# A two-layer decoder trunk on one core: when the first MLP-down weights are loaded, and where a product's addition stands in VectorE's queue

## The chip, the core and the metric

The kernel runs on one core of one Trainium2 chip. The metric is the time of one launch in microseconds (us) of device time; the figure for a kernel is the median of its runs. One further execution was taken with the profiler, and its rows are the ones read below. Engine names: PE is TensorE (matmuls), DVE is VectorE, ACT is ScalarE, POOL is GpSimd, SP is SyncE, which here only issues transfers (DMAs).

## The reference

The input x is 256 tokens by 2048 features in float32. There are two layers. Each normalises x, passes it through a token mixer (native sparse attention in layer 0, chunked gated linear attention in layer 1), adds the result to x, and then runs the part that the change touches, an MLP with a squared ReLU:

```python
def squared_relu_mlp(h, w_up, w_down):
    return jnp.square(jax.nn.relu(h @ w_up)) @ w_down

for i in range(DEPTH):
    h = rms_norm(x, norm_mix[i])
    ...
    x = x + y.astype(x.dtype)
    h = rms_norm(x, norm_mlp[i])
    x = x + squared_relu_mlp(h, mlp_w_up[i], mlp_w_down[i]).astype(x.dtype)
```

`w_up` is 2048 x 8192 and `w_down` 8192 x 2048 in each layer, all in float32.

## The kernel before, in words

**Weights and their two parts.** Every weight arrives in pieces of 128 x 2048 float32 (1 MB) and is used in two halves of 128 x 1024. For each half ACT writes a high part `wh` (a cast), DVE writes the low part `wl` (weight minus high part), and PE multiplies three ways: high by high, high by low, low by high. `Weights` (line 358) keeps this going. `next` (L489) hands out the half that is used now, and first calls `split` (L432) for the half three uses ahead (`AHEAD`, L359), which issues ACT's cast. The low part is issued later, by `lows` (L469), called from within the matmuls that use the current half. `lows` also issues what may follow a low part: the next transfer into the freed buffer, and the sums below.

**MLP-up** runs in 8 chunks of 1024 hidden columns, each 8 weight pieces, so 16 halves ("U" halves: 8 matmuls of 512 columns and 8 of 256). Pieces come through three buffers `raw`, loaded by SP (L419) as soon as a buffer is free.

**MLP-down** of a chunk, in chunks 0 to 6, is done by a scheme with seven products in place of eight (`Seven`, L863). For a group of four weight blocks a, b, c, d it uses the products `b11, d1, b22, b21, t2, d2, t4`, in this order (L306); their weights are a, b+a, d, c and further running sums of the blocks. The blocks are loaded into five buffers `sraw` by `load_group` (L425, the transfer is L326). The sums are made in place: some by DVE (L200), the others by POOL with an adding DMA from SBUF to SBUF (L337), which is issued from `after_lows` (L343) once the low parts that read the old value are done. Each product has two halves of six matmuls ("S" halves). After its second half, `product` (L873) calls `add` (L859), a DVE instruction that scales the PSUM tile and adds it to a 128 x 512 block of the residual `xt` (L204 in the profile). The products b22, t2, d2 and t4 go on in the PSUM tile of an earlier product, so their first matmul has to wait until that earlier product's `add` has read it.

**Order.** `MIXES` (L516) sets the order by hand: in a chunk, U halves of the next chunk stand between the products of this one (`"UU" + "SUSUSUSUSUUSUS"` twice, where each S is a whole product of two halves). Chunk 0 of MLP-up comes before all of this, with U halves alone; chunk 7 of MLP-down is done plainly. All engines run what stands in their own queue in the order in which the program issues it; other small work (squared ReLU, splits of the hidden values) is slipped in by `W.tick`, from planned costs.

Before chunk 0 of MLP-up, `mlp` (L771) loads the first group's four blocks and the first block of the second group at once, and issues the two sums for `d1`:

```python
weights.load_group(5)
first.sum("d1", 0)
first.sum("d1", 1)
```

Of the kernel before, what the change touches and what calls it, by code (L numbers as in the profile page):

```python
# [10 lines left out]
F32 = mybir.dt.float32  # L11
# [7 lines left out]
P = 128  # L19
T = 256  # L20
# [103 lines left out]
def trunk_kernel(ctx: ExitStack, tc: tile.TileContext, a: dict, out: bass.AP):  # L124
# [6 lines left out]
    def nm(s):  # L131
        uid[0] += 1
        return f"{s}_{uid[0]}"
# [7 lines left out]
    zpool = ctx.enter_context(tc.tile_pool(name="zpool", bufs=1))  # L141
# [16 lines left out]
    def mm(dst, lhsT, rhs, **kw):  # L158
        n = free(rhs)
        if lhsT.dtype == F32R:  # L160
            c = n / 2.4 + 3 if n >= 128 else 107.0
        else:
            c = max(4 * n / 2.4 + 3, 214.0)
        W.run("pe", c, [dst], [lhsT, rhs])
        nc.tensor.matmul(dst, lhsT, rhs, skip_group_check=True, **kw)  # L165
# [7 lines left out]
    def act(dst, src, func, bias=None, scale=None, acc=None):  # L173
        c = free(src) * 0.833 + (60 if in_psum(src) else 100)
        kw = {}
        outs = [dst]
        ins = [src]
        for k, v in (("bias", bias), ("scale", scale)):
            if v is not None:
                kw[k] = v  # L180
                if not isinstance(v, float):
                    c += 95
                    ins.append(v)
        if acc is not None:
            kw["accum_out"] = acc
            outs.append(acc)
            c += 95
        if func in (AF.Exp, AF.Ln, AF.Tanh) and (func == AF.Ln) != table[0]:
            table[0] = func == AF.Ln
            c += 1300  # L190
        W.run("act", c, outs, ins)
        nc.scalar.activation(dst, src, func, **kw)
# [5 lines left out]
    def tt(dst, x, y, op):  # L198
        W.run("dve", free(dst) * 1.042 + 75, [dst], [x, y])
        nc.vector.tensor_tensor(dst, x, y, op=op)  # L200

    def stt(dst, x, s, y, op0, op1):
        W.run("dve", free(dst) * 1.042 + 75, [dst], [x, s, y])
        nc.vector.scalar_tensor_tensor(dst, x, s, y, op0=op0, op1=op1)  # L204
# [8 lines left out]
    def vcopy(dst, src):  # L213
        W.run("dve", free(dst) * (1.042 if in_psum(src) else 0.53) + 75, [dst], [src])
        nc.vector.tensor_copy(dst, src)
# [31 lines left out]
    def aux(shape, dtype=F32):  # L247
        t = paux.tile(shape, dtype, tag="aux", name=nm("psx"))
        W.take("aux", t)
        return t  # L250

    def acc1():
        t = pacc.tile([P, 512], F32, tag="acc", name=nm("psa"))
        W.take("acc", t)
        return t
# [244 lines left out]
    weights = Weights()  # L500
# [17 lines left out]
    def mlp_items(c):  # L518
        return MIXES[SEVENS[c]]
# [159 lines left out]
    class PrepFeatures(Prep):  # L679
# [18 lines left out]

        def squares(self):
            yield 14000.0  # L700
            self.sum = zpool.tile([P, T], F32, tag="sum", name=nm("sum"))
            for kt in range(KT):
                while self.st[kt] is None or not self.st[kt]["done"]:
                    yield 0.0
                yield 0.0, {"aux": 1}
                ps = aux([P, 512])
                act(ps[:, 0:T], xs[kt], AF.Square)
                yield W.ready(ps)
                if kt:
                    tt(self.sum, self.sum, ps[:, 0:T], ALU.add)  # L710
                else:
                    vcopy(self.sum, ps[:, 0:T])
                W.give(ps, W.t["dve"])
# [57 lines left out]
    def mlp(prep, after, last):  # L771
        op = prep.op
        with tc.tile_pool(name="mlpz", bufs=1) as zp:
# [3 lines left out]
            def factors():  # L777

                ms = yield from prep.mean_squares()
                yield W.ready(ms)  # L780
                r2 = small.tile([P, 2, 16], F32, tag="r2", name=nm("r2"), bufs=1)[:, :, 0:NT]
                recip(r2[:, 0, :], ms)
                ts(r2[:, 1, :], r2[:, 0, :], -1.0, None, ALU.mult)
                fac["r2"] = r2
# [70 lines left out]
            def hidden_done():  # L855
                if last_z and not last_z[0]["done"]:
                    W.drain(last_z[0])

            def add(t, b, ps, sign=0):  # L859

                stt(xt[t][b], ps, fac["r2"][:, sign, t:t + 1], xt[t][b], ALU.mult, ALU.add)

            class Seven:  # L863
# [9 lines left out]
                def product(self, name):  # L873
                    if name in ("b11", "d1", "b21"):
                        W.wait({"acc": 1})
                        ps = acc1()
                        if name == "b11":
                            self.x = ps
                        else:
                            self.z = ps  # L880
                    else:
                        ps = self.x if name in ("t2", "d2", "t4") else self.z
                    fresh = name in ("b11", "d1", "b21")
                    for half in range(2):
                        hi, lo = weights.next()
                        for j in range(2):
                            p = 2 * half + j
                            ht = self.pairs[p][0]
                            xh, xl = ht[:, 0, self.A[name], :], ht[:, 1, self.A[name], :]
                            wh, wl = hi[:, j * 512:(j + 1) * 512], lo[:, j * 512:(j + 1) * 512]  # L890
                            mm(ps, xh, wh, start=(fresh and p == 0), stop=False)
                            mm(ps, xh, wl, start=False, stop=False)
                            mm(ps, xl, wh, start=False, stop=(p == 3))
                            if j == 0:
                                weights.lows()
                            W.tick(5000.0)
                    b = self.b
                    for t, k, sign in {"b11": [(0, 0, 0)], "d1": [(1, 1, 1)], "t2": [(0, 1, 1)], "b22": [(0, 1, 1)],
                                       "d2": [(1, 1, 1)], "b21": [(0, 0, 0)], "t4": [(1, 0, 0)]}[name]:
                        add(t, b + k, ps, sign)  # L900
                    if name in ("b22", "b21", "t4"):
                        W.give(ps, W.t["dve"])

# [30 lines left out]

            last_z = []
            weights.pool = zp
            first = weights.sloads[0][0][0]
            weights.load_group(5)
            first.sum("d1", 0)
            first.sum("d1", 1)  # L940
            W.spawn(factors())
            cur = Up(0)
            for f, half in [(0, 0), (1, 0), (0, 1), (1, 1)] + [(f, half) for f in range(2, 8) for half in range(2)]:
                cur.half(f, half)
            for c in range(8):
                items = mlp_items(c)
                nxt = Up(c + 1) if c < 7 else None
                plain = Plain(c, cur.pairs, 2 * SEVENS[c])
                n = {"U": 0, "S": 0, "C": 0}
                for it in items:  # L950
                    i = n[it]
                    n[it] += 1
                    if it == "U":
                        nxt.half(i // 2, i % 2)
                        if c == 6 and i == 15:
                            prep.free()
                    elif it == "S":
                        if i == 0:
                            hidden_done()
                        if i % 7 == 0:  # L960
                            seven = Seven(cur.pairs, 2 * (i // 7))
                        seven.product(Group.ORDER[i % 7])
                    else:
                        plain.half(i)
                cur.free()
                cur = nxt
# [844 lines left out]
    for kt in range(KT):  # L1811
        W.done[W.key(xs[kt])] = (3900.0, 6000.0, 8300.0, 10500.0, 13000.0, 13500.0, 17500.0, 18000.0)[kt // 2]
        preps[0].start(kt)
    nsa(preps[0], preps[1])
    mlp(preps[1], preps[2], False)
    gla(preps[2], preps[3])
    mlp(preps[3], None, True)


# [143 lines left out]
```

## Time and profile before

| | |
|---|---|
| median of 3 runs | 2203.72 us (2202.97, 2203.72, 2207.70) |
| the profiled execution | 2206.16 us, of which the span from the first to the last instruction is 2204.2 us |
| mean granted clock of PE | 0.996 of 2.4 GHz |
| PE busy | 2175.3 us of the span |
| DVE, ACT, POOL busy | 1743.6, 1363.9, 151.4 us |
| moved by DMA | 483.81 MB, mean 219 GB/s |

Times in the rows are counted from the span's start. A row of a list in order of time may stand for several instructions (xcount) and gives their common length; in brackets stands how long the engine was idle just before, and what ended that wait. "PE psx" matmuls are U halves here, "PE psa" matmuls are products. Matmuls overlap in the pipe, so lengths of work are best read as the distance between two starts. Layer 0's MLP runs from about 411 us, layer 1's from about 1510 us.

### The profile page before, as it was taken

Reading aid. Unit: us, or ns where it says so; the run is one execution under the profiler, and the core shown is the slowest. Engines: PE = TensorE matmul, PEld = TensorE weight load, DVE = VectorE, ACT = ScalarE, POOL = GpSimd, SP = SyncE. Lnnn points to the kernel's source line nnn. Section 1 sums busy time; section 2 is a strip of 40 time slices with the busy share of each in tenths; the row PEclk is TensorE's granted clock in tenths of the full one; section 3 lists DMA queues with packets and bytes.
Section 4 is the critical chain, followed back from the end, with each engine's and each line's share of the span. In section 5 each row is a group of like instructions: output and inputs, shape, how many; then the busy total and the mean of one; then the engine's idle time right before and its main releaser. Section 6 shows DMA issues by size and latency. Waiting matters only on the chain.

```text
span 2204.2 us, 29692 instructions
## 1 busy us (share of the span) xinstructions
PE 2175.3 (99%) x11131; PEld 1828.5 (83%) x11131; DVE 1743.6 (79%) x2369; ACT 1363.9 (62%) x2118; POOL 151.4 (7%) x189
## 2 busy tenths in 40 slices
PE   9999999999999999999999999999999999999999
PEld 7888888788888888888888888888888888888887
DVE  6687676589999999998666656655899999998985
ACT  6567776466666666666566555445666666666663
POOL 0010100001001001001000000000000110010010
PEclk9999999999999999999999999999999999999999
DMA  7653452749879879878655354457598798798784
GB/s 259 219 189 134 147 178 96 264 166 282 263 244 274 273 233 280 273 237 230 210 193 180 125 183 153 153 190 252 171 299 255 237 283 263 244 275 266 225 229 153
DMA packets 83087, 483.81 MB, mean 219 GB/s; under 512 B 10496, under 2 KB 13200, under 8 KB 35072
## 3 DMA queue, kind: packets, MB, share of 16 engines
q1 hardware_dynamic: 61264, 403.78, 49.7%
q0 software_dynamic: 21680, 78.15, 18.4%
q8 instruction: 87, 1.43, 0.2%
q14 instruction: 56, 0.46, 0.1%
HBM read 405.35 MB, written 2.10 MB: 185 GB/s over the span
## 4 chain that ended last, share of the span: by engine, by line
PE 94%; DMA 3%; DVE 2%; ACT 1%; issue 0%; SPq 0%; ACTq 0%; DVEq 0%
PE psa L165 58%; PE psx L165 34%; DMA raw<-in_mlp_up_dram 2%; PE psx L169 2%; DVE wl L200 1%; DMA sraw<-sraw 1%; ACT wh L196 0%; DMA raw<-in_nsa_in_dram 0%; DVE xt L204 0%; SPq L326 0%; DVE att L1690 0%; ACT zz L196 0%; DVE sraw L200 0%; DVE pT L200 0%; SPq L1804 0%
## 5 line engine op out<-in xcount | busy, mean ns | idle before, releaser
L165 PE MATMUL psa<-wh,op 128*128 128x512 f32 x2616 | 863.0, 394 | 1.5 <-ACT wh L196 1.5
L200 DVE TENSOR_TENSOR wl<-raw,wh 128x1024 fp32r<-128x1024 f32 (+1 forms) x529 | 641.9, 1219 | 252.6 <-ACT wh L196 248.6
L196 ACT CAST wh<-raw 128x1024 fp32r<-128x1024 f32 (+1 forms) x533 | 557.3, 1047 | 313.1 <-PE psa L165 247.0
L165 PEld LDWEIGHTS psa<-wh,op 128*128 128x128 f32 x2616 | 491.9, 188 | 107.4 <-ACT wh L196 2.5
L200 DVE TENSOR_TENSOR wl<-sraw,wh 128x1024 fp32r<-128x1024 f32 x392 | 475.0, 1221 | 83.5 <-ACT wh L196 81.9
L165 PE MATMUL psx<-op,wh 128*128 128x512 f32 (+1 forms) x2080 | 519.7, 392 | 7.6 <-ACT wh L196 7.6
L165 PE MATMUL psa<-wl,op 128*128 128x512 f32 x1308 | 510.8, 391 | 0.8 <-DVE wl L200 0.8
L196 ACT CAST wh<-sraw 128x1024 fp32r<-128x1024 f32 x392 | 409.5, 1049 | 145.5 <-PE psa L165 86.7
L165 PEld LDWEIGHTS psx<-op,wh 128*128 128x128 f32 (+1 forms) x2080 | 387.2, 189 | 87.6 <-ACT wh L196 8.0
L165 PE MATMUL psa<-wh,ht 128*128 128x512 f32 x1128 | 387.4, 396 | 11.4 <-ACT zz L196 5.5
L165 PEld LDWEIGHTS psx<-op,wl 128*128 128x128 f32 x2048 | 281.0, 191 | 20.3
L165 PE MATMUL psx<-op,wl 128*128 128x256 f32 x2048 | 287.2, 283 | 0.0
L165 PEld LDWEIGHTS psa<-wl,op 128*128 128x128 f32 x1308 | 246.2, 188 | 48.4 <-DVE wl L200 1.5
L165 PEld LDWEIGHTS psa<-wh,ht 128*128 128x128 f32 x1128 | 212.9, 189 | 57.5 <-ACT zz L196 8.4
L165 PE MATMUL psa<-wl,ht 128*128 128x512 f32 x564 | 221.9, 393 | 0.0
L337 POOL DMA_DIRECT2D sraw<-sraw x140 | 120.2, 957 | 1324.7 <-DVE pz L200 485.2
L204 DVE SCALAR_TENSOR_TENSOR xt<-psa,r,xt 128x512 f32<-128x512 f32 x212 | 157.4, 745 | 7.9 <-PE psa L165 7.9
L196 ACT COPY zz<-psx 128x256 f32<-128x256 f32 x128 | 47.7, 373 | 163.2 <-PE psx L165 163.2
L165 PEld LDWEIGHTS psa<-wl,ht 128*128 128x128 f32 x564 | 106.2, 188 | 16.9
L200 DVE TENSOR_TENSOR sraw<-sraw,sraw 128x1024 f32<-128x1024 f32 x84 | 102.6, 1221 | 1.0
L200 DVE TENSOR_TENSOR zz<-psx,zz 128x256 f32<-128x256 f32 x128 | 53.7, 420 | 11.1 <-ACT zz L196 9.9
L196 ACT CAST ht<-pz 128x896 fp32r<-128x896 f32 (+1 forms) x40 | 37.1, 928 | 25.7 <-DVE pz L204 24.7
(195 smaller groups left out, 1206.7 us busy)
## 6 DMA issues: line engine op xcount, KB each, us to landing
raw<-in_mlp_up_dram SPq DMA_DIRECT2D x128, 1024.0 KB, 8.5
sraw<-in_mlp_down_dram SPq DMA_DIRECT2D x112, 1024.0 KB, 11.0
sraw<-sraw POOLq DMA_DIRECT2D x140, 512.0 KB, 9.3
raw<-in_gla_in_dram SPq DMA_DIRECT2D x48, 1024.0 KB, 4.9
raw<-in_nsa_in_dram SPq DMA_DIRECT2D x38, 1024.0 KB, 4.9
raw<-in_nsa_out_dram SPq DMA_DIRECT2D x16, 1024.0 KB, 4.9
raw<-in_mlp_down_dram SPq DMA_DIRECT2D x16, 1024.0 KB, 4.9
raw<-in_gla_out_dram SPq DMA_DIRECT2D x16, 1024.0 KB, 4.8
```

The lines of the kernel that those rows point to most:

```text
L165: nc.tensor.matmul(dst, lhsT, rhs, skip_group_check=True, **kw)
L169: nc.tensor.transpose(dst, src, idn)
L196: nc.scalar.copy(dst, src)
L200: nc.vector.tensor_tensor(dst, x, y, op=op)
L204: nc.vector.scalar_tensor_tensor(dst, x, s, y, op0=op0, op1=op1)
L337: nc.gpsimd.dma_start(dst, src, accum_op=ALU.add)
```

## The change

Three edits. (1) In place of five transfers of MLP-down blocks ahead of chunk 0, one is issued after the second half of each of the columns f = 1 to 5 of that chunk; the two sums for `d1` follow the second of them. (2) In a product, `lows` is called in the first half where it was, but for the second half it is called after the product's `add`. (3) The 1 KB tile `sum`, used in layer 0's first norm, shares the buffer `junk`.

```diff
@@ squares (PrepFeatures)
-            self.sum = zpool.tile([P, T], F32, tag="sum", name=nm("sum"))
+            self.sum = zpool.tile([P, T], F32, tag="junk", name=nm("sum"))
@@ Seven.product
-                            if j == 0:
+                            if (half, j) == (0, 0):
                                 weights.lows()
                             W.tick(5000.0)
                     b = self.b
                     for t, k, sign in {"b11": [(0, 0, 0)], "d1": [(1, 1, 1)], "t2": [(0, 1, 1)], "b22": [(0, 1, 1)],
                                        "d2": [(1, 1, 1)], "b21": [(0, 0, 0)], "t4": [(1, 0, 0)]}[name]:
                         add(t, b + k, ps, sign)
+                    weights.lows()
                     if name in ("b22", "b21", "t4"):
                         W.give(ps, W.t["dve"])
@@ mlp
             weights.pool = zp
-            first = weights.sloads[0][0][0]
-            weights.load_group(5)
-            first.sum("d1", 0)
-            first.sum("d1", 1)
             W.spawn(factors())
             cur = Up(0)
             for f, half in [(0, 0), (1, 0), (0, 1), (1, 1)] + [(f, half) for f in range(2, 8) for half in range(2)]:
                 cur.half(f, half)
+                if half and 1 <= f <= 5:
+                    first = weights.sloads[0][0][0]
+                    weights.load_group()
+                    if f == 2:
+                        first.sum("d1", 0)
+                        first.sum("d1", 1)
```

**SP's queue at the start of layer 0's MLP** (`raw` is a piece of MLP-up, `sraw` a block of MLP-down). Before:

```order
L419 DMA raw_4246<-in_mlp_up_dram 128x2048
L326 DMA sraw_4262<-in_mlp_down_dram 128x2048
L326 DMA sraw_4264<-in_mlp_down_dram 128x2048
L326 DMA sraw_4266<-in_mlp_down_dram 128x2048
L326 DMA sraw_4268<-in_mlp_down_dram 128x2048
L326 DMA sraw_4270<-in_mlp_down_dram 128x2048
L419 DMA raw_4283<-in_mlp_up_dram 128x2048
L419 DMA raw_4349<-in_mlp_up_dram 128x2048
L419 DMA raw_4404<-in_mlp_up_dram 128x2048
```

With the change:

```order
L419 DMA raw_4246<-in_mlp_up_dram 128x2048
L419 DMA raw_4271<-in_mlp_up_dram 128x2048
L419 DMA raw_4337<-in_mlp_up_dram 128x2048
L326 DMA sraw_4382<-in_mlp_down_dram 128x2048
L419 DMA raw_4394<-in_mlp_up_dram 128x2048
L326 DMA sraw_4439<-in_mlp_down_dram 128x2048
L419 DMA raw_4453<-in_mlp_up_dram 128x2048
L326 DMA sraw_4488<-in_mlp_down_dram 128x2048
L419 DMA raw_4500<-in_mlp_up_dram 128x2048
L326 DMA sraw_4545<-in_mlp_down_dram 128x2048
L419 DMA raw_4557<-in_mlp_up_dram 128x2048
L326 DMA sraw_4592<-in_mlp_down_dram 128x2048
```

The five `sraw` transfers, which stood together ahead of the second `raw` shown, now stand singly, one behind each `raw` from the third on. Layer 1 has the same.

**DVE's queue in chunk 0 of layer 0, around product `d1`** (psa_4795 is the PSUM tile of `d1`, which `b22` goes on filling; wl_4807 is the low part of the second half of `b22`; xt is the residual). Before:

```order
L200 TENSOR_TENSOR wl_4797<-sraw_4266,wh_4796 128x1024
L200 TENSOR_TENSOR wl_4807<-sraw_4266,wh_4806 128x1024
L204 SCALAR_TENSOR_TENSOR xt_2983<-psa_4795,r_834_4380,xt_2983 128x512
L200 TENSOR_TENSOR wl_4818<-raw_4604,wh_4817 128x1024
L200 TENSOR_TENSOR wl_4839<-sraw_4268,wh_4838 128x1024
```

With the change:

```order
L200 TENSOR_TENSOR wl_4797<-sraw_4488,wh_4796 128x1024
L204 SCALAR_TENSOR_TENSOR xt_2983<-psa_4795,r_829_4368,xt_2983 128x512
L200 TENSOR_TENSOR wl_4807<-sraw_4488,wh_4806 128x1024
L200 TENSOR_TENSOR wl_4818<-raw_4604,wh_4817 128x1024
L200 TENSOR_TENSOR wl_4839<-sraw_4545,wh_4838 128x1024
```

The addition has moved ahead of one low part.

**DVE's queue in the same chunk, second group, around product `d2`** (psa_5088 is the PSUM tile of `d2` and then `t4`; wl_5358 and wl_5368 are the low parts of the two halves of `t4`). Before:

```order
L200 TENSOR_TENSOR wl_5335<-raw_5082,wh_5334 128x1024
L200 TENSOR_TENSOR wl_5358<-sraw_4270,wh_5357 128x1024
L200 TENSOR_TENSOR wl_5368<-sraw_4270,wh_5367 128x1024
L204 SCALAR_TENSOR_TENSOR xt_2991<-psa_5088,r_834_4380,xt_2991 128x512
L200 TENSOR_TENSOR wl_5383<-raw_5169,wh_5382 128x1024
```

With the change:

```order
L200 TENSOR_TENSOR wl_5335<-raw_5086,wh_5334 128x1024
L200 TENSOR_TENSOR wl_5358<-sraw_4592,wh_5357 128x1024
L204 SCALAR_TENSOR_TENSOR xt_2991<-psa_5088,r_829_4368,xt_2991 128x512
L200 TENSOR_TENSOR wl_5368<-sraw_4592,wh_5367 128x1024
L200 TENSOR_TENSOR wl_5383<-raw_5169,wh_5382 128x1024
```

Here too the addition has changed places with the low part of the second half.

## Rows read from the trace of the kernel before

**Rows 1.** part 1 of the page: each engine, busy us (share of the span) xinstructions.
```profile
PE 2175.3 (99%) x11131; PEld 1828.5 (83%) x11131; DVE 1743.6 (79%) x2369; ACT 1363.9 (62%) x2118; POOL 151.4 (7%) x189
```

**Rows 2.** the chain that ended last, in order of time: start us, us, what.
```profile
414.68 23.21 DMA raw<-in_mlp_up_dram
...
539.14 2.77 PE psa L165 x12
...
2128.08 3.04 PE psa L165 x12
```

**Rows 3.** PE in order of time, layer 0: start us, us, what xcount [idle <-releaser].
```profile
429.30 2.00 PE L165 MATMUL psx<-op,wh 128*128 128x512 f32 x8
...
432.09 2.00 PE L165 MATMUL psx<-op,wh 128*128 128x512 f32 x8
...
439.06 3.78 PE L165 MATMUL psx<-op,wh 128*128 128x512 f32 x8 [4.02 <-ACT wh L196]
...
444.17 2.00 PE L165 MATMUL psx<-op,wh 128*128 128x512 f32 x8
```

**Rows 4.** a 5 us window: each engine's busy us; then PEclk, DMA share, GB/s.
```profile
440.00:445.00 5.00, 5.00 (x19) 4.21 (x18) 5.00 (x7) 3.96 (x7) 0.00 (x0) 0.61 0.45 154
```

**Rows 5.** ACT in order of time, the same place.
```profile
437.97 1.04 ACT L196 CAST wh<-raw 128x1024 fp32r<-128x1024 f32 x1 [11.54 <-DMA raw<-in_mlp_up_dram]
```

**Rows 6.** PE in order of time, the same place of layer 1.
```profile
1530.85 2.00 PE L165 MATMUL psx<-op,wh 128*128 128x512 f32 x8
...
1537.41 3.78 PE L165 MATMUL psx<-op,wh 128*128 128x512 f32 x8 [3.61 <-ACT wh L196]
...
1542.70 2.17 PE L165 MATMUL psx<-op,wh 128*128 128x512 f32 x8
```

**Rows 7.** all engines in order of time, chunk 0 of layer 0, before product b22.
```profile
477.45 2.36 DVE L200 TENSOR_TENSOR wl<-sraw,wh 128x1024 fp32r<-128x1024 f32 x2
...
477.62 1.98 PE L165 MATMUL psx<-op,wh 128*128 128x512 f32 x8
...
479.72 0.75 DVE L204 SCALAR_TENSOR_TENSOR xt<-psa,r,xt 128x512 f32<-128x512 f32 x1
...
480.61 0.47 PE L165 MATMUL psa<-wh,ht 128*128 128x512 f32 x1
...
480.92 0.39 PE L165 MATMUL psa<-wl,ht 128*128 128x512 f32 x1
```

**Rows 8.** all engines, the same chunk, before the second group's product t4.
```profile
541.75 1.98 PE L165 MATMUL psx<-op,wh 128*128 128x512 f32 x8
542.01 2.36 DVE L200 TENSOR_TENSOR wl<-sraw,wh 128x1024 fp32r<-128x1024 f32 x2
...
544.28 0.74 DVE L204 SCALAR_TENSOR_TENSOR xt<-psa,r,xt 128x512 f32<-128x512 f32 x1
...
545.17 0.47 PE L165 MATMUL psa<-wh,ht 128*128 128x512 f32 x1 [0.49 <-ACT zz L196]
```

**Rows 9.** tile raw, 547 to 1040 us: its DMAs' last line.
```profile
DMA to landing us min/median/max: 4.7/8.7/12.5
```

**Rows 10.** all engines, chunk 1 of layer 0, product b22 and what follows.
```profile
567.69 1.22 DVE L200 TENSOR_TENSOR wl<-sraw,wh 128x1024 fp32r<-128x1024 f32 x1
567.75 1.98 PE L165 MATMUL psx<-op,wh 128*128 128x512 f32 x8
...
568.82 0.75 DVE L204 SCALAR_TENSOR_TENSOR xt<-psa,r,xt 128x512 f32<-128x512 f32 x1
...
569.48 1.21 DVE L200 TENSOR_TENSOR wl<-raw,wh 128x1024 fp32r<-128x1024 f32 x1
```

**Rows 11.** the window of chunk 1 of layer 0, columns as in group 4.
```profile
547.90:632.30 84.40, 83.81 (x427) 71.13 (x426) 77.82 (x89) 55.69 (x64) 8.54 (x10) 1.00 0.85 263
```

**Rows 12.** all engines, chunk 5 of layer 1, a late sum.
```profile
2034.49 1.05 ACT L196 CAST wh<-sraw 128x1024 fp32r<-128x1024 f32 x1 [1.97 <-DMA sraw<-sraw]
...
2043.00 0.47 PE L165 MATMUL psa<-wh,ht 128*128 128x512 f32 x1 [1.36 <-DVE xt L204]
```

## The prediction

> **What bounds the kernel now.** I read the page's busy times first, then the chain that ended last, then PE's list in order of time at each place where that chain leaves PE. PE is busy for 2175.3 of 2204.2 us and DVE, the next, for 1743.6 [rows 1]. So PE sets the end, and an edit gains only what it takes out of PE's stops and slow stretches. The chain shows two kinds of them in the MLPs. The long one is a transfer of an MLP-up piece, 23.21 us from issue to landing [rows 2]; the least for such a piece later in the MLP is 4.7 us [rows 9]. The short ones are stops before a product; the last of them ends at 2128.08 [rows 2], and the first two are at 480.61 and 545.17 [rows 7, 8]. All of layer 0's and layer 1's chunks 0 to 6 have these two short stops each, 28 in all.
>
> **The change, part by part.**
>
> *The loads, the long stop.* In SP's queue before, five 1 MB blocks of MLP-down stand ahead of one piece of MLP-up, as the order of SP shows. That piece is issued at 414.68 and lands 23.21 us later [rows 2], at 437.89. ACT has stood idle for 11.54 us when its cast starts at 437.97 [rows 5], so the piece was due at 426.4, 11.7 us after its issue. PE stops until the cast is done. Two U halves start 2.79 us apart when nothing is wrong (429.30 to 432.09). The one from 432.09 is followed only at 439.06, 6.97 us later, so 4.18 are lost. The next, from 439.06 to 444.17, takes 5.11, so 2.32 more are lost [rows 3]: the granted clock is 0.61 on average from 440 to 445 us [rows 4], that is partly at the lower level of 1.2 GHz, after PE had idled for 4.02 us. Layer 0 loses 6.50 us. In layer 1 the same two halves take 6.56 and 5.29 us [rows 6], so 3.77 and 2.50 are lost, 6.27 us. Together 12.8 us.
>
> With the change the same `raw` is issued where it was, with nothing ahead of it but another `raw`. Each later `raw` has one block before it, and the pieces of f = 4 to 7 meet the two sums of `d1` too, which wait for the second block and so start later than before. This mix of one piece, one block and two sums is not in the trace at this place, so I bound it: pieces between 547 and 1040 us, which fly among blocks and sums, land in 4.7 to 12.5 us, median 8.7 [rows 9]. A piece is due after 11.7 us, and PE did not stop at once when one was late: 11.54 us of lateness cost it 4.02 us of idling, so 7.5 us of lateness are absorbed by the halves already prepared. Even 12.5 us leaves PE running. From the other side, the gain cannot exceed the 12.8 us that are lost. I take the whole, as the worst row is 0.8 us late against 7.5 absorbed. The blocks themselves get later by 9 to 30 us, but the first product comes only after the 16 U halves of chunk 0 and two more; its cast, three halves ahead, is due 15 x 2.79 = 42 us after the MLP's start near 411. At one block for two halves (5.6 us), the second is issued near 427 us and the fifth, which belongs to the second group, near 444. The U halves hide them all.
>
> *The addition ahead of a low part, the short stops.* Before b22 (chunk 0) the U half takes 2.99 us from 477.62 to 480.61, 0.20 too long, and the first matmul of the product 0.31 to the next in place of 0.23 (2.77 us for 12 [rows 2]), 0.08 more: 0.28 us [rows 7]. Before the second group's t4 the U half takes 3.42 us, 0.63 too long, and 0.08 again (also 0.47 long): 0.71 us [rows 8]. PE waits there for DVE's addition to have read the PSUM tile. For t4 the list names ACT's copy to zz as what ended the wait; but in both places PE starts 0.14 to 0.15 us after the end of the addition (480.47 and 545.02), and the copy has no part in the product's operands. In both, the product had ended near the start of the U half, and the addition stood behind two low parts, 2.36 us of DVE [rows 7, 8].
>
> With the change it stands behind one. Before b22 it starts at 478.6 and ends at 479.3, and b22 can start at 480.41 without a wait. Before t4 it runs from 543.1 to 543.9, and t4 can start at 544.54. Both stops go: 0.99 us for each chunk, in 7 chunks of 2 layers, 13.9 us.
>
> *What the moved low part costs.* It ends 0.67 us later where DVE is behind. The tightest of the rows: the second low of 542.01 to 544.37 would end at 545.0 [rows 8]; it is used in the second half of t4, at 544.54 + 6 x 0.23 + 0.23 = 546.2. So 1.1 us are left. Where DVE is not behind, it loses time: the low of 567.69 ran while the product's last matmuls were still running, as the next U half starts at 567.75 [rows 10]. With the change DVE waits until about 568.0, adds until 568.7, and the low after that ends near 569.8, so the next low starts 0.3 us later than 569.48 [rows 10]. If all 14 products of a chunk lost 0.3 us, that would be 4.2 us; DVE has 84.40 - 77.82 = 6.6 us free in a chunk [rows 11]. So I cost it at nothing; if DVE had no free time, it would be up to 14 x 4.2 = 59 us. The Trainium skill (PSUM — Partial Sum Buffer, section Engine vs sequencer instructions) says that VectorE's queue is strictly first in, first out: by it an addition at the head holds back every low part behind it until its product has ended. By the rule the 0.3 us are thus lost at every product, and if nothing covered them the gain would be turned into a loss; by the rows DVE's free time covers them and the sum stays as it is. The sums and loads issued after a moved low part start 0.3 to 0.7 us later in POOL's and SP's queues; rival three prices that.
>
> *The tile `sum`* is read by PE long before `junk` is written again, and no order but DVE's and SP's changes near it: nothing.
>
> **The sum.** 12.8 + 13.9 = 26.7 us. The profiled execution took 2206.16 us, its span 2204.2; 26.7 off gives 2179.5. It is 2.4 us above the median of the runs, and holds a stop of 1.36 us behind a late sum [rows 12] that other chunks lack. From the median of 2203.72 I get 2177.0 us. Alone, this case spans 2172 (late sums rarer, as an addition no longer waits behind their low part) to 2184 (half of the short stops left).
>
> **The rivals.**
>
> *One: only the loads pay.* The short stops stay, because the wait is on something else (the list does name ACT for t4) or because the low parts held back [rows 10] stop PE as long as the additions did. For it: that name. Against: the 0.15 us in both places, the 1.1 us of margin. Time: 2203.7 - 12.8 = 2190.9.
>
> *Two: only the additions pay.* Pieces of MLP-up, now each behind a block and among sums, land late again. PE stops from 11.7 + 7.5 = 19.2 us after issue on; the rows have 12.5 at most [rows 9]. Time: 2203.7 - 13.9 = 2189.8.
>
> *Three, slower: late sums.* POOL's adding DMAs are issued after the low parts that the change delays. A cast waited 1.97 us for such a sum, and the next stop of PE was 1.36 us [rows 12]. So about 0.6 us of lateness is absorbed, and from there on PE pays. If the delay of up to 0.7 us, met by busier DMA engines, set off such a stop in each of the 28 groups, it would cost 38 us: 2177 + 38 = 2215. Against: it takes casts that already wait for their sum in every group, and the trace has this rarely.
>
> *Four: no change.* PE's lost time comes back in full elsewhere, as DMA or DVE would bound the MLP. Against it: in a chunk the DMA share is 0.85, and DVE is busy for 77.8 of 84.4 us [rows 11]. Time: 2203.7.
>
> **How the numbers follow.** Forecast 0.80, rival one 0.07, two 0.06, three 0.04, four 0.03. The range of 2171 to 2187 holds the forecast with its bounds and 1 us of spread on the low side, 3 on the high; rivals one to four lie outside, 2 in 10. About 0.2% (4.4 us) is what a measurement can tell from no change; so faster by more is 0.80 + 0.07 + 0.06 = 0.93, the same 0.03, slower 0.04.
>
> **What would show it.** Right: no transfer of MLP-up over 13 us at the start of either MLP, U halves 2.79 us apart through chunk 0, and the granted clock at full there; no matmul of 0.47 us before b22 or the second t4; chunks 83.4 us long in place of 84.4. Wrong: PE's waits before products kept with an addition long done (rival one); a stop in chunk 0 with ACT waiting for `raw` (two); many casts waiting for sums, and stops of a microsecond or more behind them (three).

## The result and the profile after

The change takes the median from 2204.14 us (4 runs, 2202.97 to 2207.70) to 2179.36 us (4 runs, 2175.89 to 2180.12): a ratio of 0.9882, 95% interval 0.9865 to 0.9899. The gain is 24.8 us (22.3 to 29.8 by the interval) where 26.7 were forecast, and the time lies 2.4 us above the 2177.0 of the prediction, inside its range. The profiled execution is the fastest of the four, 2175.89 us, with a span of 2174.1.

Part 1 of the page of the changed kernel, to be read beside [rows 1]:

```profile
PE 2162.6 (99%) x11131; PEld 1821.0 (84%) x11131; DVE 1742.7 (80%) x2369; ACT 1363.7 (63%) x2118; POOL 151.4 (7%) x189
```

The work is the same, instruction for instruction; only the waits went. PE in order of time at the start of layer 0's MLP, where [rows 3] had the long stop (start us, us, what):

```profile
428.86 2.00 PE L165 MATMUL psx<-op,wh 128*128 128x512 f32 x8
...
431.65 2.00 PE L165 MATMUL psx<-op,wh 128*128 128x512 f32 x8
...
434.45 2.00 PE L165 MATMUL psx<-op,wh 128*128 128x512 f32 x8
...
437.24 2.00 PE L165 MATMUL psx<-op,wh 128*128 128x512 f32 x8
...
440.03 2.00 PE L165 MATMUL psx<-op,wh 128*128 128x512 f32 x8
```

The U halves start 2.79 us apart throughout. The window of [rows 4] (busy us by engine, then PEclk, DMA share, GB/s) and the last line of tile `raw` from 411 to 460 us:

```profile
440.00:445.00 5.00, 5.00 (x29) 4.33 (x28) 3.31 (x4) 2.38 (x3) 0.00 (x0) 1.00 1.04 295
```

```profile
DMA to landing us min/median/max: 4.9/5.0/10.9
```

The granted clock is 1.00 where it was 0.61. The latest piece of MLP-up flies for 10.9 us, less than the 11.7 after which it is due, although DMA is busier here than before (0.45 in [rows 4]).

All engines in order of time ahead of product b22, the place of [rows 7]:

```profile
470.52 1.22 DVE L200 TENSOR_TENSOR wl<-sraw,wh 128x1024 fp32r<-128x1024 f32 x1
...
470.69 1.98 PE L165 MATMUL psx<-op,wh 128*128 128x512 f32 x8
...
471.66 0.74 DVE L204 SCALAR_TENSOR_TENSOR xt<-psa,r,xt 128x512 f32<-128x512 f32 x1
...
473.46 0.39 PE L165 MATMUL psa<-wh,ht 128*128 128x512 f32 x1
```

and ahead of the second group's t4, the place of [rows 8]:

```profile
534.78 1.98 PE L165 MATMUL psx<-op,wh 128*128 128x512 f32 x8
...
536.17 0.75 DVE L204 SCALAR_TENSOR_TENSOR xt<-psa,r,xt 128x512 f32<-128x512 f32 x1
...
536.83 1.22 DVE L200 TENSOR_TENSOR wl<-sraw,wh 128x1024 fp32r<-128x1024 f32 x1
...
537.54 0.39 PE L165 MATMUL psa<-wh,ht 128*128 128x512 f32 x1
```

The addition starts 0.97 and 1.39 us into the U half where it stood at 2.10 and 2.53, the U halves are 2.77 and 2.76 us long instead of 2.99 and 3.42, and the product's first matmul takes 0.39 in place of 0.47. From the b22 at 473.46 to that of the next chunk at 556.95 are 83.5 us, and the chunk after takes 83.1; before it was 84.3 and 84.1.

What is left shows in the chain that ended last (start us, us, what). No transfer of MLP-up stands in the MLP's part of it any more, but two other transfers do:

```profile
896.02 8.37 DMA sraw<-in_mlp_down_dram
905.55 16.86 DMA sraw<-sraw
929.20 2.99 PE psa L165 x12
```

A block of MLP-down, then an adding DMA of `d1`, lead to a product that takes 2.99 us instead of 2.77. The experiments turn on this.

### The profile page after: what moved, and what is told of

It reads as the page before. It is cut to its first block, busy times and chain, and to the rows that moved or that the text cites. A ratio compares the mean times of both kernels' runs of the same rounds, so it can differ in the third digit from the quotient of the medians.

```text
span 2174.1 us, 29700 instructions
## 1 busy us (share of the span) xinstructions
PE 2162.6 (99%) x11131; PEld 1821.0 (84%) x11131; DVE 1742.7 (80%) x2369; ACT 1363.7 (63%) x2118; POOL 151.4 (7%) x189
## 3 DMA queue, kind: packets, MB, share of 16 engines
q0 software_dynamic: 21680, 78.15, 18.1%
## 4 chain that ended last, share of the span: by engine, by line
PE 97%; DMA 2%; DVE 1%; ACT 0%; SPq 0%; issue 0%; POOL 0%; POOLq 0%; ACTq 0%; DVEq 0%
PE psa L165 58%; PE psx L165 37%; PE psx L169 2%; DMA sraw<-sraw 1%; DMA raw<-in_nsa_in_dram 1%; DMA sraw<-in_mlp_down_dram 0%; DVE wl L200 0%; ACT wh L196 0%; DVE att L1693 0%; SPq L1807 0%; DVE pT L200 0%; ACT p L192 0%; SPq L411 0%; ACT pT L196 0%; DVE xt L204 0%
## 5 line engine op out<-in xcount | busy, mean ns | idle before, releaser
L200 DVE TENSOR_TENSOR zz<-psx,zz 128x256 f32<-128x256 f32 x128 | 53.6, 419 | 14.5 <-ACT zz L196 14.5
```

## The experiments

The diffs stand against the changed kernel. For every run I name **PE's lost time**: over the trace, what the distance between two matmul starts exceeds its usual length by (0.23 us for 512 columns), where that is over 0.1 us. "Chunk 0" is from 412 to 460 and 1512 to 1560 us, "rest" what follows to the end of each layer. The ratio is to the runs of before on the same chip, in the same set (medians 2204.14, 2205.42, 2205.07 and 2202.76 us for the sets that begin with the rows "after", "change again", "additions alone" and "loads alone, a earlier"). "Late casts" is the row of the waits view for ACT's cast `wh` behind `DMA sraw<-sraw`: us in total, times.

| run | loads spread | new order in | block a behind | median us | ratio [95%] | chunk 0 | rest | late casts |
|---|---|---|---|---|---|---|---|---|
| before | no | none | t2 | 2204.1 | 1 | 11.6 | 16.2 | 11.1, 6 |
| after | yes | all | t2 | 2179.36 | 0.9882 [0.9865, 0.9899] | 0 | 1.6 | 22.4, 12 |
| change again | yes | all | t2 | 2179.56 | 0.9881 [0.9865, 0.9896] | 0 | 7.2 | 44.0, 19 |
| loads alone | yes | none | t2 | 2190.48 | 0.9940 [0.9924, 0.9955] | 0 | 13.6 | 10.1, 9 |
| d1, d2 | yes | d1, d2 | t2 | 2184.53 | 0.9904 [0.9891, 0.9918] | 0 | 10.1 | 39.0, 17 |
| the others | yes | the others | t2 | 2204.20 | 1.0004 [0.9992, 1.0015] | 0 | 26.5 | 36.1, 17 |
| additions alone | no | all | t2 | 2190.85 | 0.9940 [0.9926, 0.9953] | 10.4 | 5.6 | 39.9, 19 |
| burst behind f = 1 | at once, later | all | t2 | 2183.35 | 0.9905 [0.9891, 0.9918] | 4.7 | 5.3 | 34.2, 17 |
| a earlier | yes | all | b21 | 2173.92 | 0.9863 [0.9850, 0.9877] | 0 | 0.3 | 6.9, 4 |
| a and sum earlier | yes | all | b21 | 2173.78 | 0.9861 [0.9848, 0.9875] | 0 | 0 | 4.2, 2 |
| loads alone, a earlier | yes | none | b21 | 2187.05 | 0.9925 [0.9910, 0.9940] | 0 | 11.1 | none |
| d1, d2, a earlier | yes | d1, d2 | b21 | 2174.16 | 0.9867 [0.9846, 0.9887] | 0 | 0 | none |
| the others, a earlier | yes | the others | b21 | 2189.72 | 0.9934 [0.9918, 0.9951] | 0 | 12.9 | 4.1, 2 |
| own tile for sum, a earlier | yes | all | b21 | 2173.98 | 0.9867 [0.9849, 0.9885] | 0 | 0 | 5.9, 4 |

**The change again.** No edit; a second profiled execution, and a value to set the others against.

> The changed kernel once more, for a second profiled execution and as the yardstick of the three beside it. My theory (two separate gains, 12.8 us from the loads, 13.9 us from the additions) and the rival (the additions gain nothing of their own) both expect the time measured before, 2176 to 2180 us. If late sums are what sets its executions apart, a slower profile shows casts waiting for sums and stops of PE of some tenths to 2 us behind them, and nothing else that differs.

2179.56 us. This profiled execution took 2183.05, and 7.2 us of stops are in it where the first had 1.6. So executions of the changed kernel differ among themselves, behind chunk 0 of the MLPs.

**The loads alone.**

```diff
-                            if (half, j) == (0, 0):
+                            if j == 0:
                                 weights.lows()
...
                         add(t, b + k, ps, sign)
-                    weights.lows()
```

> The loads are spread; the additions stand where they stood before. Theory: only the long stops go, 12.8 us, so 2204.1 - 12.8 = 2191.3 us, and the 28 short stops of 0.28 and 0.71 us stay. Rival one (the short stops were not the additions' doing): 2179 us, as fast as the full change. Rival two (the loads gain nothing): 2204 us.

2190.48 us. The stop in chunk 0 and the lower clock are gone from the trace, the short stops ahead of b22 and t4 are there. They are 26 and not 28: the last chunk of each layer has none ahead of t4. Five more stops, 2.6 us together, stand ahead of the second group's b22.

**The new order in d1 and d2 alone, and in the others alone.** The two runs differ in one word:

```diff
-                            if (half, j) == (0, 0):
+                            if (half, j) == (0, 0) or (j == 0 and name not in ("d1", "d2")):
```

with `in` for `not in` in the second.

> The loads are spread; the addition precedes the last low part only in the products d1 and d2, whose PSUM tile is taken up again after one U half. Theory: these two make both short stops of a chunk, so the time is that of the full change, 2179 us within 2 us. Rival (the low parts held back in the other five products cost time): faster than the full change by 2 us or more. Rival (the other additions gain too): slower than the full change, up to 2191 us.

> The loads are spread; the addition precedes the last low part in all products but d1 and d2. Theory: the 28 short stops stay, 2191 us, like the loads alone. Rival (it is DVE's order at large that counts): between 2179 and 2187 us.

Both missed. With d1 and d2 alone (2184.53) the short stops are gone, but new ones of 0.2 to 1.0 us stand ahead of the second group's b22 in 11 of the 14 chunks; the time lies where the rival had put it by which the other additions gain too, and a run below decides on that. With the others alone (2204.20) they stay, and new ones of up to 1.46 us come on top: 13.7 us worse than moving no addition at all. So the forecast had named the two additions behind the short stops, and not what moving the others, or leaving them, does elsewhere.

All engines of the run with the others moved, in chunk 1 of layer 0 (start us, us, what [idle before <- what ended it]):

```profile
590.57 0.75 DVE L204 SCALAR_TENSOR_TENSOR xt<-psa,r,xt 128x512 f32<-128x512 f32 x1
...
592.53 1.05 ACT L196 CAST wh<-sraw 128x1024 fp32r<-128x1024 f32 x1 [3.00 <-DMA sraw<-sraw]
...
593.61 1.23 DVE L200 TENSOR_TENSOR wl<-sraw,wh 128x1024 fp32r<-128x1024 f32 x1 [2.29 <-ACT wh L196]
...
596.15 1.99 PE L165 MATMUL psx<-op,wh 128*128 128x512 f32 x8
...
596.89 2.36 DVE L200 TENSOR_TENSOR wl<-sraw,wh 128x1024 fp32r<-128x1024 f32 x2
...
599.50 0.74 DVE L204 SCALAR_TENSOR_TENSOR xt<-psa,r,xt 128x512 f32<-128x512 f32 x1
...
600.39 0.47 PE L165 MATMUL psa<-wh,ht 128*128 128x512 f32 x1 [1.30 <-DVE xt L204]
```

ACT's cast for the second half of d1 (second group) waits 3.00 us for an adding DMA. Its low part waits 2.29 us at the head of DVE's queue, and all behind it is late; d1's addition, which in this run stands behind two more low parts, ends at 600.24, and b22 starts 0.15 us after it. The U half before it takes 4.24 us in place of 2.77: 1.5 us late. The same stretch of the whole change, run again:

```profile
588.92 0.74 DVE L204 SCALAR_TENSOR_TENSOR xt<-psa,r,xt 128x512 f32<-128x512 f32 x1
...
590.36 1.05 ACT L196 CAST wh<-sraw 128x1024 fp32r<-128x1024 f32 x1 [2.48 <-DMA sraw<-sraw]
...
591.44 1.22 DVE L200 TENSOR_TENSOR wl<-sraw,wh 128x1024 fp32r<-128x1024 f32 x1 [1.78 <-ACT wh L196]
...
594.08 1.99 PE L165 MATMUL psx<-op,wh 128*128 128x512 f32 x8
...
594.72 1.22 DVE L200 TENSOR_TENSOR wl<-sraw,wh 128x1024 fp32r<-128x1024 f32 x1
...
596.19 0.74 DVE L204 SCALAR_TENSOR_TENSOR xt<-psa,r,xt 128x512 f32<-128x512 f32 x1
...
597.07 0.48 PE L165 MATMUL psa<-wh,ht 128*128 128x512 f32 x1
```

The cast is late by 2.48 us, but b11's addition is done before the wait and d1's stands behind one low part fewer; the U half takes 2.99 us, so 0.22 us are lost and not 1.5. With d1 and d2 alone, b11's addition stands behind the low part that waits, and up to 1.0 us is lost. Late sums are thus rival three at work, and the order of all seven products sets what each costs.

**The additions alone; the five loads at once, but later.** In the first run the burst is back ahead of chunk 0 (and the five lines in the loop over f are gone):

```diff
             weights.pool = zp
+            first = weights.sloads[0][0][0]
+            weights.load_group(5)
+            first.sum("d1", 0)
+            first.sum("d1", 1)
             W.spawn(factors())
```

In the second:

```diff
-                if half and 1 <= f <= 5:
+                if half and f == 1:
                     first = weights.sloads[0][0][0]
-                    weights.load_group()
-                    if f == 2:
-                        first.sum("d1", 0)
-                        first.sum("d1", 1)
+                    weights.load_group(5)
+                    first.sum("d1", 0)
+                    first.sum("d1", 1)
```

> The five loads stand again in one go ahead of the first chunk of MLP-up; every product keeps the new order, its second half's additions ahead of the low part. If the two parts of the change act in places that do not touch, their gains add: the loads alone took 14.9 us off (2205.4 to 2190.5), the whole change 25.9 (to 2179.6), so the additions alone take off 11 and this run gives 2194 +- 2, with the 3.8 us stop and the granted clock near 0.6 behind it in chunk 0 of layer 0 as before, and the stops ahead of the second group's t4 gone. If instead the additions are worth the 13.9 us that the forecast gave them, whatever the loads do, it gives 2190 to 2192. If they only pay once the loads are spread, over 2200.

> The whole change, but the five loads and the two adding DMAs of d1 are issued together once the second half of f = 1 is done, not one by one. The first theory is that spreading is what pays: a load of MLP-up queued behind five blocks lands 23.2 us after its issue, late by 3.8 us wherever in chunk 0 the five stand, so the stop of 3.8 us and the lower clock behind it come back in both layers and the time is 2190 to 2194. The rival: it is the place that pays, since behind f = 1 the pieces of MLP-up ahead in the queue have landed and the next one is due some 19 us after its issue; then a stop of at most 2 us in each layer is left, and the time is 2179 to 2184. A third: no stop at all, 2179.5 +- 1.5.

The additions alone give 2190.85 us. That is below the 2194 of strict addition, by about the width of the intervals, so additivity is neither shown nor refuted. The long stop is there as in before. PE in order of time, and the window of [rows 4]:

```profile
431.02 2.00 PE L165 MATMUL psx<-op,wh 128*128 128x512 f32 x8
...
437.95 3.30 PE L165 MATMUL psx<-op,wh 128*128 128x512 f32 x8 [3.98 <-ACT wh L196]
...
442.42 2.00 PE L165 MATMUL psx<-op,wh 128*128 128x512 f32 x8
```

```profile
440.00:445.00 5.00, 5.00 (x26) 4.37 (x26) 4.74 (x8) 3.96 (x6) 0.00 (x0) 0.80 0.52 172
```

The burst behind f = 1 (2183.35 us) fits its rival, a stop of about 2 us in each layer (2.35 in the second). All engines at its stop, and the window that holds it:

```profile
446.85 1.04 ACT L196 CAST wh<-raw 128x1024 fp32r<-128x1024 f32 x1 [9.50 <-DMA raw<-in_mlp_up_dram]
...
447.95 2.11 PE L165 MATMUL psx<-op,wh 128*128 128x512 f32 x8 [1.98 <-ACT wh L196]
...
450.85 1.32 PE L165 MATMUL psx<-op,wh 128*128 128x512 f32 x5
```

```profile
446.00:451.00 5.00, 3.05 (x17) 2.71 (x18) 3.07 (x4) 4.15 (x6) 0.00 (x0) 1.00 0.86 361
```

The `raw` behind the five blocks flies for 20.5 us; ACT waits 9.50 and PE stops for 1.98, so 7.5 us are absorbed, as the forecast read from [rows 3, 5]. The clock stays at 1.00 and the next half takes 2.90 us. So by the trace a later place brings most of the gain of the loads, and spreading them the last 2.2 to 2.5 us of each layer; the median is 3.8 us above that of the change run again, with intervals some 3 us wide on either side.

**The next group's block a one product earlier.** This is the test of the late sums. SP loads the second group's block a behind a piece of MLP-up, POOL issues the two sums of `d1` once a has landed, and ACT's cast needs the second of them. The edit moves the load alone:

```diff
-            if piece in ("t2", "d2"):
+            if piece in ("b21", "d2"):
                 weights.load_group()
```

and the second run also writes the sums one product earlier:

```diff
-            if piece == "d2" and self.next is not None:
+            if piece == "t2" and self.next is not None:
```

> The whole change, and the next group's block a is loaded behind the low parts of b21 and not of t2, one product earlier; its sums of d1 stay where they are written but can start when a has landed. If the stops left before the second group's b22 (0.2 to 0.4 us each, 1 us at worst, 1 to 5 us in a layer) come from the adding DMA of that group's d1 being late for ACT's cast, the cast's waits of 2 to 3 us go, the stops with them, and the time is 2174 to 2178, with less spread between executions. If they come from VectorE's queue being full there whatever the sums do, nothing changes: 2179.5 +- 1.5. If the earlier load holds back a load of MLP-up, which it now stands ahead of, a stop on a tile raw appears once a chunk: 2182 or more.

> As the run before, and the next group's sums of d1 are also written one product earlier, behind the low parts of t2 and not of d2. If POOL's order already lets them start when block a has landed, this equals the run before within 1.5 us. If what is written ahead of them held them back, their landing comes earlier still and the time is below it. If four adding DMAs at once slow the sums of t4, which are needed first, ACT's cast for t4 waits and stops appear ahead of t4: 2181 or more.

2173.92 and 2173.78 us: the faster end, and the two agree. Of PE's stops in the MLPs one of 0.21 us is left in the first trace and none over 0.15 in the second; these are the best versions of the study. SP and POOL in order of time in chunk 1, of the run with the load alone moved (a row of x3 stands for three issues):

```profile
556.90 0.33 SPq L326 DMA_DIRECT2D sraw<-in_mlp_down_dram  x1
...
569.79 2.60 POOL L337 DMA_DIRECT2D sraw<-sraw  x3 [3.08 <-ACT wh L196]
```

and of the change again:

```profile
562.90 1.22 DVE L200 TENSOR_TENSOR wl<-raw,wh 128x1024 fp32r<-128x1024 f32 x1
...
564.15 0.33 SPq L419 DMA_DIRECT2D raw<-in_mlp_up_dram  x1
...
564.53 0.42 SPq L326 DMA_DIRECT2D sraw<-in_mlp_down_dram  x1
...
573.41 1.73 POOL L337 DMA_DIRECT2D sraw<-sraw  x2 [1.48 <-DMA sraw<-in_mlp_down_dram]
...
573.84 0.33 SPq L419 DMA_DIRECT2D raw<-in_mlp_up_dram  x1
```

and of before, where [rows 10] end:

```profile
570.72 0.33 SPq L419 DMA_DIRECT2D raw<-in_mlp_up_dram  x1
...
571.10 0.42 SPq L326 DMA_DIRECT2D sraw<-in_mlp_down_dram  x1
...
579.91 1.72 POOL L337 DMA_DIRECT2D sraw<-sraw  x2 [1.73 <-DMA sraw<-in_mlp_down_dram]
...
580.75 0.33 SPq L419 DMA_DIRECT2D raw<-in_mlp_up_dram  x1
```

In before, the next `raw` leaves 9.65 us after block a, and 0.31 us behind POOL's second sum (it starts at 580.44 inside the row of two). That sum lands 13.5 us after its issue, 0.7 us before the cast. With the change the `raw` leaves 9.31 us after block a, and 0.11 us ahead of the second sum (573.95). The sum lands 16.3 us after its issue, and the cast waits 2.48 us. With the earlier block a the load has landed at 561.8, so the two sums of `d1` follow the sum for t4 at once (the row of three; they start at 570.37 and 570.91), 13 to 14 us behind the load's issue in place of 9, and the next `raw` leaves at 572.55, 1.6 us behind the second. The second lands after 12.8 us, 2.8 us before the cast.

Over the 14 chunks of the eight traces with block a behind t2 this is nearly a rule: where the `raw` was issued ahead of the second sum, the cast waited over 1.5 us in 67 of 71 cases, where behind it in 2 of 41. In before it was ahead in 3 of 14, in the change again in all 14 (13 late). The distance from block a to that `raw` is 9.63 us at the median in before, 9.32 with the change. The 0.3 us are those that the prediction found in [rows 10]: the low part that frees the `raw` ahead of block a starts at 562.90, 2.05 us into its U half, where before it started 1.73 us into it. Block a stands behind that `raw`; the next `raw` is not delayed, since DVE has made up the time by then. They are not the whole of it: block a lands 7.9 us after its issue at the median in before, 8.0 in the first trace of the change and 8.3 in the second, and the second sum is issued about 1.2 us after that landing in all three. This is where the two traces of the change differ, with the `raw` ahead in 6 and in 14 chunks; why block a lands later was not tried.

**What each part is worth without late sums.** The same block a, with the edits of "the loads alone", "d1 and d2 alone" and "the others alone" from above, and, with the full order, with the tile `sum` in its own memory:

```diff
-            self.sum = zpool.tile([P, T], F32, tag="junk", name=nm("sum"))
+            self.sum = zpool.tile([P, T], F32, tag="sum", name=nm("sum"))
```

> The loads of the first group spread, the old order of the additions, and the next group's block a loaded behind b21. This measures the additions without the late sums: set against the run with the whole change and the earlier block a (2173.9), it lacks the additions' new order alone. If that order is worth the 13.9 us of the forecast (14 stops of 0.28 and 14 of 0.71 us), it gives 2187.8 +- 1.5, with those 28 stops in its trace and no other. If the old order had no late sums to lose it stays at the 2190.5 of the loads alone.

> Only the products d1 and d2 in the new order, and the next group's block a loaded behind b21. If the 5 us by which d1 and d2 alone fell behind the whole change came from the second group's sums of d1 landing late, they go: 2174 +- 1.5 and no stops in MLP, so that d1 and d2 are all that the order is worth, as the forecast had it. If they came from the low parts of b11 and of the others standing where they stood, the time stays near 2184.5.

> Only the products other than d1 and d2 in the new order, and the next group's block a loaded behind b21. By the first theory (late sums) the 13 us by which this order fell behind the loads alone go, and the 28 short stops stay: 2187.8 +- 1.5. If the order of the others itself holds VectorE back, it stays near 2204.

> The whole change with block a loaded behind b21, but the tile sum of squares has its own memory again, as before. The forecast costs this edit at nothing: 2173.9 +- 1. If sharing the memory of junk made squares wait, this is faster by more than 1 us.

The loads alone come down by 3.4 us to 2187.05; its trace has the 26 short stops, no other in the MLPs, and no late cast. Against the full order in the same set of runs (2173.98, with the tile of its own) the additions are worth 13.1 us; 13.9 were forecast. With d1 and d2 alone it is 2174.16 and no stop over 0.15 us in the MLPs: those two are all that the order is worth, and the other additions gain nothing. The others alone give 2189.72, near the loads alone and 14.5 us below what the same order gave with block a behind t2. Of the 2.7 us that it lies above them the trace shows 1.8 us in one stop, in the last chunk, behind a late cast for t4. The tile `sum` is worth nothing, as forecast.

## Why the prediction was right, and which term was off

**The loads: right.** 12.8 us were forecast. The loads alone took off 14.9 (2205.42 to 2190.48, an interval some 3 us wide on either side), and between the additions alone and the whole change, from two sets of runs, lie 11.3; 12.8 is between them. The mechanism held: transfers of 4.9 to 10.9 us, no stop, full clock, and PE's lost time in chunk 0 down from 11.6 us to none. The 7.5 us that the prepared halves absorb came out the same in the burst behind f = 1.

**The additions: right in place, one count too high.** They stop PE by way of d1 and d2 alone, and are worth 13.1 us. The prediction counted 28 stops; there are 14 ahead of b22 and 12 ahead of t4, which at its prices make 14 x 0.28 + 12 x 0.71 = 12.4 us. The stop that it took for the last of them (2128.08 in [rows 2]) stands ahead of the second group's b22, 7.5 us behind a cast that waited 2.94 us for a sum of `d1`: it belonged to the late sums.

**The moved low part: set at nothing, with one path left out of the sum.** The prediction saw that DVE loses 0.3 us per product, saw that DVE has 6.6 us free in a chunk to cover it, and set the cost at nothing. DVE did cover it, so that PE was not held by it. But SP issues `raw` and block a behind that low part, and these 0.3 us are as much as the margin by which POOL's second sum was ahead of the next `raw` (0.31 in the chunk shown). Casts that wait over 1.5 us for the second sum of `d1` stand in 3 of 14 chunks in before and in 2 with the loads alone, but in 6 and 13 in the two traces of the change. The Trainium skill (PSUM — Partial Sum Buffer, section Engine vs sequencer instructions), with its VectorE queue in strict order, agrees with the trace in a second place too: the late low part at the queue's head holds the additions behind it for as long as it waits, 1.78 and 2.29 us above.

What this costs is less sure. The medians put late sums at 3.4 us in the old order (2190.48 to 2187.05) and at 5.6 in the new one (2179.56 to 2173.92); by the ratios, each against the before of its own set, it is 3.3 and 4.0, and each ratio is uncertain by some 3 us. PE's lost time gives 5.1 us in before (16.2 less the 11.1 of the short stops) and 2.5 with the loads alone, against 1.6 and 7.2 in the two traces of the change. So it is shown that late sums hold up the changed kernel, and not shown that they cost it more than they cost before. The 1.9 us by which the gain fell short of the forecast lie within its interval, and no term can be blamed for them. That the number came out so close is in part luck: the sum holds neither the late sums of before, but for the 2.4 us by which it set off the profiled execution, nor those that the change keeps, and the two are of like size. An estimate from the traces: 2204.1 less 12.8 for the loads, 12.4 for the 26 stops and 5.1 for the late sums is 2173.8, where the versions without late sums of `d1` lie (2173.78 to 2174.16).

**The rivals.** One and two were priced well, 2190.9 and 2189.8 us, and the loads and the additions alone give 2190.48 and 2190.85; both parts pay, so neither is the case. Three was right as a mechanism and wrong twice in size. A late cast is not rare: before's own trace has one in 3 of 14 chunks, and the change up to 13 of 14 in one execution. And in that execution they go with 7.2 us of stops, about half a microsecond each and not 1.36. In nine of the chunks 0.2 to 0.3 us are lost ahead of b22, because the additions no longer stand behind the low part that waits; where the cast waits longest, `d1` itself stops for that low part (1.5 us behind the wait of 3.87 at 1929.83). In another order a late cast does cost what the rival said: with only the other five moved, they ate the whole gain of the loads (2204.20). Four is refuted.

**Still open.** No run changed only which of `raw` and second sum is issued first; the earlier block a also gives the sums 3 us. So it is shown that late sums cause the remaining stops, while the part of the order of the two issues rests on the counts above.

## What to carry to other kernels

When an instruction is delayed at no cost to its own engine, follow what is issued behind it: here a load that left 0.3 us later went with a sum that was issued behind another transfer and landed some 2.8 us later (16.3 against 13.5). When a chain of load, sum and cast ends within a microsecond of its use, start its head earlier before reordering anything near it; here one product earlier was worth another 4.0 to 5.6 us, and the executions agreed better: 2173.23 to 2176.11 us in four of them, where the change took 2175.89 to 2183.05 in eight. And when an edit acts at many places, run it at the places you credit and at the others apart: the sum can hide one that loses.

## What the runs showed of the hardware that was not expected

- **The order of two issues.** In the eight traces with block a behind t2 the second adding DMA of `d1` (512 KB) took 13.5 to 16.0 us from issue to landing with the 1 MB `raw` issued behind it (41 cases); with the `raw` ahead of it, be it by 0.1 us, 13.8 to 18.1 (71 cases), median 16.4 against 14.3. No run changed this order alone.
- **The clock after a stop.** After PE had idled for 3.98 us, the granted clock was 0.80 from 440 to 445 us, that is partly at the lower of its two levels (1.2 GHz), and the half behind the stop took 4.47 us; after 1.98 us it was 1.00 (2.4 GHz), and that half took 2.90. With the halves' own 2.79 us taken off, half the stop cost 2.2 us in all where the whole cost 5.8.
- **Late casts are cheap or dear by what stands behind them.** 44.0 us of waiting in the change again went with 7.2 us of stops; 36.1 us with the others moved, with 26.5, of which some 11 are the short stops.
